# Low parts of every second w_up tile formed by an accumulating DMA in SBUF

## Chip, cores and metric

The kernel runs on one core of one Trainium2 chip. The metric is the device time of one execution in microseconds (us), from two runs of the kernel before.

## What is computed

The reference is one decoder layer in float32: x is 256 tokens of 2048 features; attention and a gated short convolution run side by side, then comes cross-attention on 256 memory tokens, a squared-ReLU MLP and a final norm. The change lies in the MLP's first product:

```
u = jax.nn.relu(rms_norm(x, norm_mlp) @ w_up)      # w_up: 2048 x 8192
x = x + (u * u) @ w_down                           # w_down: 8192 x 2048
```

The inputs and the weights are float32, and the output has to be near a float32 result.

## The kernel before

TensorE multiplies in the format float32r (F32R), which keeps fewer bits than float32. So each operand is split: a high part, which is the value rounded to F32R, and a low part, which is what the rounding left. A product is then formed from three matmuls: high by high, high by low, low by high.

Weights stream from HBM. `weights` (L70) loads a tile of 256 rows by 512 columns (512 KB; in SBUF 128 partitions by 1024 elements) with one DMA from SP's queue (`load_w`, L54 to L59) into a buffer `raw`, and splits it (`split_w`, L61 to L68): ScalarE writes `whi`, the rounded weights (L66), and VectorE writes `wlo` = raw - whi (L67). There are six `raw` buffers and five each of `whi` and `wlo` (L40, L41). A buffer is filled anew when the last reader of its former content is done. SP's queue issues the loads in order, so a load that waits for its buffer holds back those behind it.

The MLP works in four passes (L468). Each first forms 2048 of the 8192 hidden features with w_up, in four groups of 512 columns (`feat_group`, L84 to L94), and then multiplies them with 2048 rows of w_down into the token-major residual (`tok_group`, L107 to L114), four groups again. In `feat_group` the contraction over 2048 rows runs in four steps of four k tiles (L87): two tiles of weights are loaded and split (L88), and for each of four blocks of 128 output features four k tiles go through `feat_step`. Here the weights are the operand that TensorE loads, and the activations move through. For each k one matmul has the high weights and 512 columns, the activations' high and low parts side by side (L78), and one has the low weights and 256 columns (L79); for a group's last k the order is turned round (L81, L82). At a group's end ScalarE and VectorE evacuate each block as it is finished (`ev_u`, L473 to L479), square it and split it for the next product.

So w_up takes 16 groups of four steps, and each step uses two loaded tiles, which `split_w` returns as four (high, low) pairs. The framework puts in the semaphores, and orders each engine's instructions by its own simulated schedule.

Of the kernel before, what the change touches and what calls it, by code (L numbers as in the profile page):

```python
# [11 lines left out]
F32R = mybir.dt.float32r  # L12
AF = mybir.ActivationFunctionType
ALU = mybir.AluOpType
# [3 lines left out]
P = 128  # L18
# [16 lines left out]
def hybrid_block(ctx: ExitStack, tc: tile.TileContext, x, mem, xf, memf, cols, rope, w_in, w_attn_out,  # L35
                 w_conv_out, w_mix_out, wq_x, wkv_x, wo_x, w_up, w_down, norm_final, out):
    nc = tc.nc
# [3 lines left out]
    wsp = ctx.enter_context(tc.tile_pool(name="wsp", bufs=5))  # L41
# [5 lines left out]
    def psum_mm():  # L47
        return mm.tile([P, 512], F32, name="acc")
# [5 lines left out]
    def load_w(w, k0, nk, c0, step=2):  # L54
        raw = wraw.tile([P, nk, 512], F32, name="raw")
        for k in range(0, nk, step):
            rows = w[(k0 + k) * P:(k0 + k + step) * P, c0:c0 + 512]
            nc.sync.dma_start(raw[:, k:k + step, :], rows.rearrange("(k p) c -> p k c", p=P))
        return raw  # L59

    def split_w(raw, hi=None, lo=None, step=2):  # L61
        nk = raw.shape[1]
        hi = wsp.tile([P, nk, 512], F32R, name="whi") if hi is None else hi
        lo = wsp.tile([P, nk, 512], F32R, name="wlo") if lo is None else lo
        for k in range(0, nk, step):
            nc.scalar.activation(hi[:, k:k + step, :], raw[:, k:k + step, :], AF.Copy)  # L66
            nc.vector.tensor_sub(lo[:, k:k + step, :], raw[:, k:k + step, :], hi[:, k:k + step, :].bitcast(F32))  # L67
        return [(hi[:, k, :], lo[:, k, :]) for k in range(nk)]  # L68

    def weights(w, k0, c0):  # L70
        return split_w(load_w(w, k0, 2, c0))


    def feat_step(ps, b, k, nk, wh, wl, xs):

        a, c = wh[:, b * P:(b + 1) * P], wl[:, b * P:(b + 1) * P]
        if k < nk - 1:
            nc.tensor.matmul(ps, a, xs(k, 2), start=(k == 0), stop=False)  # L78
            nc.tensor.matmul(ps[:, S:], c, xs(k, 0), start=False, stop=False)  # L79
        else:  # L80
            nc.tensor.matmul(ps[:, S:], c, xs(k, 0), start=False, stop=False)  # L81
            nc.tensor.matmul(ps, a, xs(k, 2), start=(k == 0), stop=True)  # L82

    def feat_group(w, c0, kr0, nk, xs, evac):  # L84

        ps = [None] * 4
        for k0 in range(0, nk, 4):  # L87
            parts = weights(w, kr0 + k0, c0) + weights(w, kr0 + k0 + 2, c0)  # L88
            for b in range(4):
                ps[b] = psum_mm() if k0 == 0 else ps[b]  # L90
                for j in range(4):
                    feat_step(ps[b], b, k0 + j, nk, *parts[j], xs)
                if k0 + 4 == nk:
                    evac(b, ps[b])  # L94
# [21 lines left out]
    def parts_of(t, k0=0):  # L116

        def get(k, which):
            if which == 2:
                return t[:, k0 + k, :, :].rearrange("p a s -> p (a s)")  # L120
            return t[:, k0 + k, which, :]
        return get
# [35 lines left out]
    for q in range(8):  # L158
        raw = wraw.tile([P, 2, 512], F32, name="raw") if q < 6 else None
# [69 lines left out]
    for c in range(2):  # L229
        for i in range(2):  # L230
# [5 lines left out]
            if i == c == 0:  # L236
                ps = [psum_mm(), psum_mm()]
                for q in range(8):
                    for k in range(2):
                        split_scaled(hT, 2 * q + k, xraw[:, 2 * q + k, :], g_of(0, 2 * q + k))  # L240
                    parts = split_w(first[q] or load_w(w_in, 2 * q, 2, 0), step=1 if q < 2 else 2)
# [162 lines left out]
    for h in range(NX):  # L404
# [6 lines left out]
        for c in range(2):  # L411
            nc.scalar.activation(px[:, h, c, :], sc[:, c * S:(c + 1) * S], AF.Exp, bias=st[:, 2 + c:3 + c],
                                 scale=SCALE, accum_out=st[:, 4 + c:5 + c])
# [5 lines left out]
    for k0 in range(0, KD, 4):  # L419
        parts = weights(wkv_x, k0, 512) + weights(wkv_x, k0 + 2, 512)  # L420
# [47 lines left out]
    for g in range(NG):  # L468
        uT = big.tile([P, KG, 2, S], F32R, name="S2")
        for j in range(FG // 512):  # L470
            z = block().rearrange("p a (b s) -> p (a b) s", s=S)

            def ev_u(b, ps, j=j, uT=uT, z=z):  # L473
                nc.scalar.activation(z[:, b, :], ps[:, S:], AF.Copy)  # L474
                nc.vector.tensor_add(z[:, b, :], ps[:, :S], z[:, b, :])  # L475
                if b % 2:
                    t = z[:, b - 1:b + 1, :]
                    nc.vector.scalar_tensor_tensor(t, t, 0.0, t, op0=ALU.max, op1=ALU.mult)  # L478
                    split_act(uT, 4 * j + b - 1, t, 2)  # L479
            feat_group(w_up, g * FG + j * 512, 0, KD, parts_of(x3g), ev_u)  # L480
        for c in range(4 if g < NG - 1 else 3):
            def ev_d(h, ps, c=c, g=g):
                if g < NG - 1:
                    add_block(h, ps, c * 512, 512)
                else:
                    add_last(h, ps, c * 512, 512, c, nc.gpsimd)
            tok_group(w_down, c * 512, g * KG, KG, parts_of(uT), ev_d)
# [4 lines left out]
    c0, kr, xu = 1536, (NG - 1) * KG, parts_of(uT)  # L492
    ps = [psum_mm() for _ in range(3)]
    cuts = ((0, ps[0], 0, 512), (1, ps[1], 0, 256), (1, ps[2], 256, 256))
    for k0 in range(0, 8, 4):
        parts = weights(w_down, kr + k0, c0) + weights(w_down, kr + k0 + 2, c0)
        for h, t, o, n in cuts:
            tok_steps(t[:, :n], h, k0, KG, parts, xu, o, n)
    parts = []
# [65 lines left out]
```

## Time and profile before

| What | us |
|---|---|
| median of two runs | 1476.82 |
| lowest, highest run | 1476.53, 1477.11 |
| the profiled execution | 1476.77 |
| its span, first to last instruction | 1475.0 |

The profile tells one execution. Busy time says how long an engine worked on instructions; the time of a DMA is told by its issue on a queue, by the share of time in which the core's 16 DMA engines were busy, and by the bytes they moved. PE is TensorE's matmul, PEld its weight load, DVE is VectorE, ACT is ScalarE, POOL is GpSimd, SPq is the queue of SyncE. An idle time in square brackets at a row's end names what the engine waited for last. An engine that is idle and isn't on the path that sets the end costs nothing.

### The profile page before, as it was taken

To read this page: it belongs to the slowest core of one execution; us is meant where nothing else is said; L and a number is where in the kernel's file an instruction comes from. 1 tells how busy PE (TensorE), PEld (TensorE's weight loads), DVE (VectorE), ACT (ScalarE), POOL (GpSimd) and SP (SyncE) were. 2 spreads that over 40 slices of the span, in tenths; PEclk is the share of its full clock that TensorE was granted. 3 is DMA by queue.
4 is the path that set the end of the run, shared out by engine and by line. 5 is a ranking of instruction groups with operands and counts; after the bars stand their busy time and mean duration, and the time that the engine had idled before them with its cause. 6 is when DMAs were issued, how large, how long until landed. Compare 5 with 4: busy or idle time off the path is not lost.

```text
span 1475.0 us, 18233 instructions
## 1 busy us (share of the span) xinstructions
PE 1454.8 (99%) x7064; PEld 1222.4 (83%) x7064; DVE 820.9 (56%) x976; ACT 691.2 (47%) x905; POOL 13.6 (1%) x21
## 2 busy tenths in 40 slices
PE   6999999999999999999999999999999999999997
PEld 5888888888888888888888888888888888888886
DVE  5545555765554646654476655556545555556554
ACT  6444544454444445554564443444434443445442
POOL 0000000000000000000000000000000000000011
PEclk9999999999999999999999999999999999999999
DMA  9666655576666667655555566565565556665652
GB/s 337 193 193 180 184 165 178 170 227 190 187 196 188 186 197 230 212 192 180 172 171 185 187 198 191 182 197 180 194 200 179 193 188 191 192 191 179 198 189 85
DMA packets 145158, 281.27 MB, mean 191 GB/s; under 512 B 8880, under 2 KB 9520, under 8 KB 144944
## 3 DMA queue, kind: packets, MB, share of 16 engines
q1 hardware_dynamic: 141888, 272.66, 58.9%
q10 hardware_dynamic: 3184, 7.45, 1.5%
q8 instruction: 55, 0.90, 0.2%
q14 instruction: 31, 0.25, 0.1%
HBM read 277.98 MB, written 2.10 MB: 190 GB/s over the span
## 4 chain that ended last, share of the span: by engine, by line
PE 98%; DMA 1%; ACT 1%; issue 0%; DVE 0%; POOLq 0%; POOL 0%; DVEq 0%; SPq 0%; ACTq 0%
PE acc L104 23%; PE acc L105 23%; PE acc L103 23%; PE acc L78 15%; PE acc L79 8%; PE aps L145 1%; PE acc L82 1%; DMA tok<-in_x_dram 1%; PE acc L81 1%; DMA raw<-in_w_in_dram 0%; ACT junk L189 0%; PE aps L315 0%; PE aps L270 0%; PE aps L438 0%; PE aps L407 0%
## 5 line engine op out<-in xcount | busy, mean ns | idle before, releaser
L67 DVE TENSOR_TENSOR wlo<-raw,whi 128x1024 fp32r<-128x1024 f32 (+1 forms) x510 | 618.7, 1222 | 561.2 <-ACT whi L66 547.5
L66 ACT ACTIVATE whi<-raw 128x1024 fp32r<-128x1024 f32 (+1 forms) x510 | 532.9, 1055 | 564.1 <-PE acc L105 386.2
L103 PE MATMUL acc<-whi,S 128*128 128x512 f32 x1512 | 584.9, 388 | 11.4 <-ACT whi L66 11.4
L105 PE MATMUL acc<-whi,S 128*128 128x512 f32 x1512 | 587.9, 389 | 0.0
L104 PE MATMUL acc<-wlo,S 128*128 128x512 f32 x1512 | 586.3, 388 | 0.3 <-DVE wlo L67 0.3
L103 PEld LDWEIGHTS acc<-whi,S 128*128 128x128 f32 x1512 | 284.6, 188 | 68.8 <-ACT whi L66 12.7
L78 PE MATMUL acc<-S,whi 128*128 128x512 f32 x960 | 341.6, 398 | 0.0
L104 PEld LDWEIGHTS acc<-wlo,S 128*128 128x128 f32 x1512 | 284.5, 188 | 58.8 <-DVE wlo L67 1.6
L105 PEld LDWEIGHTS acc<-whi,S 128*128 128x128 f32 x1512 | 284.7, 188 | 56.2
L79 PE MATMUL acc<-S,wlo 128*128 128x256 f32 x960 | 269.7, 281 | 0.0
L78 PEld LDWEIGHTS acc<-S,whi 128*128 128x128 f32 x960 | 180.4, 188 | 41.3
L79 PEld LDWEIGHTS acc<-S,wlo 128*128 128x128 f32 x960 | 181.3, 189 | 3.1
L474 ACT ACTIVATE blk<-acc 128x256 f32<-128x256 f32 x64 | 24.3, 380 | 36.0 <-PE acc L82 35.8
L189 ACT ACTIVATE junk<-tok 128x512 f32<-128x512 f32 (+1 forms) x33 | 20.2, 613 | 37.7 <-DVE tok L459 23.6
L459 DVE SCALAR_TENSOR_TENSOR tok<-acc,q,tok 128x512 f32<-128x512 f32 (+1 forms) x33 | 24.1, 731 | 18.0 <-PE acc L105 18.0
L130 ACT ACTIVATE S<-blk 128x512 fp32r<-128x512 f32 x32 | 20.0, 626 | 25.7 <-DVE blk L478 25.7
L475 DVE TENSOR_TENSOR blk<-acc,blk 128x256 f32<-128x256 f32 x64 | 27.0, 422 | 8.0 <-ACT blk L474 8.0
L131 DVE TENSOR_TENSOR S<-blk,S 128x512 fp32r<-128x512 f32 x32 | 22.1, 692 | 9.9 <-ACT S L130 8.4
L82 PE MATMUL acc<-S,whi 128*128 128x512 f32 x64 | 25.6, 400 | 0.0
L478 DVE SCALAR_TENSOR_TENSOR blk<-blk 128x512 f32<-128x512 f32 x32 | 22.0, 689 | 0.6
L204 ACT ACTIVATE blk<-acc,r 128x512 f32<-128x512 f32 x18 | 12.4, 689 | 15.5 <-PE acc L105 15.5
L81 PE MATMUL acc<-S,wlo 128*128 128x256 f32 x64 | 18.1, 283 | 0.0
(127 smaller groups left out, 466.2 us busy)
## 6 DMA issues: line engine op xcount, KB each, us to landing
raw<-in_w_in_dram SPq DMA_DIRECT2D x158, 512.0 KB, 4.2
raw<-in_w_up_dram SPq DMA_DIRECT2D x128, 512.0 KB, 4.0
raw<-in_w_down_dram SPq DMA_DIRECT2D x128, 512.0 KB, 4.3
raw<-in_w_mix_out_dram SPq DMA_DIRECT2D x32, 512.0 KB, 4.9
raw<-in_w_attn_out_dram SPq DMA_DIRECT2D x16, 512.0 KB, 4.3
raw<-in_w_conv_out_dram SPq DMA_DIRECT2D x16, 512.0 KB, 4.5
raw<-in_wkv_x_dram SPq DMA_DIRECT2D x16, 512.0 KB, 4.2
raw<-in_wq_x_dram SPq DMA_DIRECT2D x8, 512.0 KB, 3.9
```

The costliest lines, as they stand in the source:

```text
L66: nc.scalar.activation(hi[:, k:k + step, :], raw[:, k:k + step, :], AF.Copy)
L67: nc.vector.tensor_sub(lo[:, k:k + step, :], raw[:, k:k + step, :], hi[:, k:k + step, :].bitcast(F32))
L78: nc.tensor.matmul(ps, a, xs(k, 2), start=(k == 0), stop=False)
L79: nc.tensor.matmul(ps[:, S:], c, xs(k, 0), start=False, stop=False)
L81: nc.tensor.matmul(ps[:, S:], c, xs(k, 0), start=False, stop=False)
L82: nc.tensor.matmul(ps, a, xs(k, 2), start=(k == 0), stop=True)
L103: nc.tensor.matmul(ps, xh, wh, start=(k == 0), stop=False)
L104: nc.tensor.matmul(ps, xh, wl, start=False, stop=False)
L105: nc.tensor.matmul(ps, xl, wh, start=False, stop=(k == nk - 1))
L459: nc.vector.scalar_tensor_tensor(t, ps, q3[:, h:h + 1], t, op0=ALU.mult, op1=ALU.add)
L474: nc.scalar.activation(z[:, b, :], ps[:, S:], AF.Copy)
L475: nc.vector.tensor_add(z[:, b, :], ps[:, :S], z[:, b, :])
```

## The change

A second way to form the two parts, `weights_added`, takes the place of `weights` for the second tile of each step of `feat_group`, that is, for every second tile of w_up. The tile is loaded as before. ScalarE first writes the rounding of the negated weights into `lo`. A DMA issued from GpSimd's queue then adds the raw weights to `lo` in SBUF, so that `lo` holds raw minus rounded; VectorE has no part in it. ScalarE writes `hi` as before, with an instruction of its own behind the negation. The first tile of each step, and all tiles of every other weight, go through `weights` as before.

```diff
+    def weights_added(w, k0, c0):
+
+        raw = load_w(w, k0, 2, c0)
+        hi = wsp.tile([P, 2, 512], F32R, name="whi")
+        lo = wsp.tile([P, 2, 512], F32R, name="wlo")
+        nc.scalar.activation(lo, raw, AF.Copy, scale=-1.0)
+        nc.gpsimd.dma_start(lo, raw, accum_op=ALU.add)
+        nc.scalar.activation(hi, raw, AF.Copy)
+        return [(hi[:, k, :], lo[:, k, :]) for k in range(2)]
+
 
     def feat_step(ps, b, k, nk, wh, wl, xs):
 
@@ -85,7 +95,7 @@
 
         ps = [None] * 4
         for k0 in range(0, nk, 4):
-            parts = weights(w, kr0 + k0, c0) + weights(w, kr0 + k0 + 2, c0)
+            parts = weights(w, kr0 + k0, c0) + weights_added(w, kr0 + k0 + 2, c0)
             for b in range(4):
```

## Rows read from the trace of the kernel before

**Rows 1.** Page, section 1: busy us, share of the span and instructions of each engine.
```profile
span 1475.0 us, 18233 instructions
PE 1454.8 (99%) x7064; PEld 1222.4 (83%) x7064; DVE 820.9 (56%) x976; ACT 691.2 (47%) x905; POOL 13.6 (1%) x21
```

**Rows 2.** Page, section 4: the chain that ended last, by engine.
```profile
PE 98%; DMA 1%; ACT 1%; issue 0%; DVE 0%; POOLq 0%; POOL 0%; DVEq 0%; SPq 0%; ACTq 0%
```

**Rows 3.** Windows view: length, busy us by engine, granted clock, DMA share, GB/s.
```profile
774.00:865.00 91.00, 91.00 (x493) 78.16 (x492) 56.18 (x66) 42.20 (x57) 0.00 (x0) 1.00 0.58 186
...
800.90:823.50 22.60, 22.60 (x130) 19.59 (x128) 13.62 (x17) 10.48 (x15) 0.00 (x0) 1.00 0.57 183
```

**Rows 4.** Timeline of ACT, 795 to 825: start us, duration us, instruction, count, idle before.
```profile
796.84 0.38 ACT L474 ACTIVATE blk<-acc 128x256 f32<-128x256 f32 x1 [0.18 <-PE acc L82]
...
801.42 0.37 ACT L474 ACTIVATE blk<-acc 128x256 f32<-128x256 f32 x1
...
805.95 2.01 ACT L66 ACTIVATE whi<-raw 128x1024 fp32r<-128x1024 f32 x2 [0.43 <-PE acc L78]
811.61 2.01 ACT L66 ACTIVATE whi<-raw 128x1024 fp32r<-128x1024 f32 x2 [3.65 <-issue]
...
819.46 0.38 ACT L474 ACTIVATE blk<-acc 128x256 f32<-128x256 f32 x1 [0.18 <-PE acc L82]
```

**Rows 5.** Timeline of PE and its weight loads, 800 to 813.6.
```profile
800.65 0.40 PE L82 MATMUL acc<-S,whi 128*128 128x512 f32 x1
800.88 0.40 PE L78 MATMUL acc<-S,whi 128*128 128x512 f32 x1
...
812.18 0.40 PE L78 MATMUL acc<-S,whi 128*128 128x512 f32 x1
...
812.89 0.19 PEld L79 LDWEIGHTS acc<-S,wlo 128*128 128x128 f32 x1
```

**Rows 6.** Timeline of DVE, 795 to 825: the two subtractions after 805.95.
```profile
807.04 2.36 DVE L67 TENSOR_TENSOR wlo<-raw,whi 128x1024 fp32r<-128x1024 f32 x2 [0.80 <-ACT whi L66]
```

**Rows 7.** Timeline of SP, 808 to 810, and all waits of SP's queue for L67.
```profile
808.30 0.37 SPq L58 DMA_DIRECT2D raw<-in_w_up_dram  x1
...
809.43 0.37 SPq L58 DMA_DIRECT2D raw<-in_w_up_dram  x1
...
SPq L58 <- DVE wlo L67: 1016.4, 431, 8.4
```

**Rows 8.** Windows of half a us behind those two issues, columns as in rows 3.
```profile
808.50:809.00 0.50, 0.50 (x4) 0.42 (x3) 0.50 (x1) 0.00 (x0) 0.00 (x0) 1.00 0.00 0
809.00:809.50 0.50, 0.50 (x5) 0.45 (x4) 0.40 (x1) 0.00 (x0) 0.00 (x0) 1.00 0.42 57
809.50:810.00 0.50, 0.50 (x5) 0.41 (x4) 0.00 (x0) 0.00 (x0) 0.00 (x0) 1.00 0.91 156
...
810.50:811.00 0.50, 0.50 (x4) 0.41 (x3) 0.00 (x0) 0.00 (x0) 0.00 (x0) 1.00 1.02 397
...
813.00:813.50 0.50, 0.50 (x5) 0.41 (x4) 0.50 (x1) 0.50 (x1) 0.00 (x0) 1.00 0.08 29
```

**Rows 9.** DMA views: w_up loads of all; packets 774 to 865; landing there.
```profile
raw<-in_w_up_dram SPq DMA_DIRECT2D x128, 512.0 KB, 4.0
...
q1 hardware_dynamic: 8733, 16.84, 57.9%
...
DMA to landing us min/median/max: 3.6/4.3/5.2
```

**Rows 10.** Lines view, 774 to 865: busy us, mean ns of one, idle before.
```profile
L67 DVE TENSOR_TENSOR wlo<-raw,whi 128x1024 fp32r<-128x1024 f32 x34 | 40.7, 1222 | 33.5 <-ACT whi L66 33.2
...
L66 ACT ACTIVATE whi<-raw 128x1024 fp32r<-128x1024 f32 x33 | 33.9, 1054 | 32.1 <-issue 27.3 <-PE acc L105 3.6 <-PE acc L78 1.3
```

**Rows 11.** POOL's own work: one line's instruction with its start, and its longest.
```profile
L197 POOL TENSOR_TENSOR rm<-rmss,mhalf x1: 688/688/688, 657.3 to 657.3; 128x2 f32<-128x2 f32 x1
...
L466 POOL TENSOR_TENSOR tok<-tok,S 128x512 f32<-128x512 f32 x6 | 8.2, 1369 | 785.1 <-ACT junk L189 785.1
```

**Rows 12.** Windows at the kernel's start, columns as in rows 3.
```profile
12.00:18.00 6.00, 2.63 (x8) 1.67 (x8) 1.57 (x3) 5.24 (x16) 0.00 (x0) 0.55 1.04 361
...
24.00:36.00 12.00, 12.00 (x54) 9.94 (x53) 10.63 (x14) 9.21 (x13) 0.00 (x0) 1.00 1.03 371
```

## Prediction

> **What bounds the kernel now.** I read the page first. The span is 1475.0 us, TensorE is busy for 1454.8 us of it, and the chain of work that ended last is TensorE for 98% [rows 1, 2]; VectorE and ScalarE are busy 56% and 47%. So taking work from VectorE can bring something only where TensorE waits for it. The windows view asks that of the stage that changes: in one group of w_up, 800.90 to 823.50, TensorE is busy for 22.60 of 22.60 us, at a granted clock of 1.00 (the 2.4 GHz level), while the DMA engines are busy 0.57 of the time [rows 3]. There is nothing to win there. The question is only whether TensorE keeps being fed.
>
> The timelines show the margin. I call the four k tiles of one pass of `feat_group`, two loaded tiles, a set. The evacuation of block 0 comes at 796.84 and one group later at 819.46 [rows 4]: 22.62 us for four sets, 5.655 us each. One set begins at 800.88, behind the last matmul of the group before [rows 5]; the second set after it begins at 812.18. Buffers are five deep and a set uses two, so the second tile of the set of 812.18 takes the buffer that the first tile of the set of 800.88 gives back shortly before that set ends. ScalarE's pair of roundings at 805.95 is just that: the first of its two activations is for the second tile of the set of 812.18, the next is for the set after [rows 4]. VectorE subtracts from 807.04, two in 2.36 us [rows 6], so the low part is there at 808.27. TensorE first loads it at 812.89, the weight load of L79 at the third k [rows 5]. The margin today is 812.89 - 808.27 = 4.6 us. The tile with this margin is the very one that the change alters.
>
> **The change part by part.** Half of the 128 loads of w_up [rows 9] are odd tiles: 64, one in each of 64 sets.
>
> Removed: 64 subtractions of 1222 ns on VectorE [rows 10], 78 us. VectorE is off the path, so this is worth nothing.
>
> Added on ScalarE: 64 negated roundings. They have the shape of the present rounding, 1054 ns [rows 10], 67 us in all. In a group ScalarE is busy 10.48 of 22.60 us [rows 3]; four more make 14.7 us, which TensorE's work covers. Behind the negation stand the same tile's rounding (805.95 plus two activations of 1.05 is 808.05, needed at 812.89), the next tile's rounding (to about 809.1, then a subtraction of 1.2, needed a set later), and at a group's end the evacuation that today starts at 801.42, about 1 us later; five accumulators leave it most of a group. I cost all these at nothing. Without the cover it would be the 67 us.
>
> Added on the DMA engines: 64 transfers from SBUF to SBUF which read 512 KB of raw weights, read 512 KB of negated high parts and write 512 KB. They are issued from POOL's queue, which does no other work between 658 us and the last group of w_down (its six products of L466 are there [rows 11]), so nothing is queued behind the wait that it gets. Two limits follow.
>
> First limit, **engine time**. With loads alone the DMA engines are busy 0.57 x 5.655 = 3.2 us per set (57.9% over a longer stretch: 3.27 us [rows 9]), 1.64 us for each of two loads. Left are 5.655 - 3.27 = 2.38 us. No row shows an adding transfer. From below, it costs the same as one load, 1.64 us, if the second read is hidden beside the first. From above, a load that runs alone shows engines 91% busy at 156 GB/s (809.5 to 810.0), against 397 GB/s with two in flight [rows 8]; two reads of 524 KB at 156 GB/s are 6.7 us. Between these I take two reads at a load's ordinary price, 3.28 us: the transfer moves two operands in for each one out, and its reads can be kept in flight as those of a load are. Then a set needs 3.27 + 3.28 = 6.55 us of the DMA engines, 0.90 us more than TensorE takes. The Trainium skill says of another use of the same adder (Collectives: The Full Stack, section "The bandwidth ceiling: the fold count and why AG ≠ RS ≠ AR") that a reducing transfer needs two source reads and so runs at half a copy's rate; by that the sum would be this one, and no run here has shown it yet.
>
> Second limit, **lateness**. The negation ends at 805.95 + 1.05 = 807.00 and the sum must have landed at 812.89: 5.9 us are free. From the issue of a load at 808.30 [rows 7] to the first bytes takes 0.7 to 1.2 us (nothing moves from 808.5 to 809.0 [rows 8]); two loads are in by about 813.0. So an add lands after 0.8 us to first bytes, its data, and some 0.3 us at the end; to that comes POOL's own preparation, which no row shows: I take 0.5 us, between nothing and the 1.37 us of its longest instruction [rows 11]. With 3.28 us of data that is 4.9 us alone. It won't be alone. SP today waits for the subtraction before it reloads a raw tile [rows 7]; for an odd tile it now waits for the add's landing, and the even tile's load stands behind it in SP's queue. So both loads start when the add lands, near 812, just as the next set's add is issued (807.00 + 5.655 = 812.66). Sharing evenly doubles the add's time at worst: 0.8 + 0.5 + 6.56 + 0.3 = 8.2 us. As the loop goes over two sets, a lateness D costs (D - 5.9)/2 per set: 1.1 us at 8.2, nothing at 4.9. The engine-time limit of 0.90 us lies inside this, at D = 7.7. The later loads themselves don't stall anything: a raw tile is wanted three sets on (805.95 + 17.0 = 822.9), ten us after 812.9, and the longest landing seen is 5.2 us [rows 9].
>
> Sum: 64 x 0.90 = 58 us, and the rest nothing. No work absorbs it, since TensorE has no idle time in these stages to give back. The profiled execution took 1476.77 us (span 1475.0 and 1.8 around it), as good as the median of 1476.82. 1477 + 58 = 1535.
>
> **The rivals.** *The add is hidden* (not slower). Place: the 42% of the DMA engines' time that is idle in w_up. If one add takes at most 2.38 us of the engines and lands within 5.9 us, nothing moves: 1477. Up to 2.84 us the cost stays under 2% (2.84 - 2.38 = 0.46 us, by 64 is 29.5 us). For it: both operands lie in SBUF, and loads at 397 GB/s [rows 8] show what the engines can carry; two reads at that rate take 2.64 us, 17 us in all, 1494. Against it: a share of 0.58 at 186 GB/s, the steady state of this stage [rows 3], is far from that rate, and the loads and the add will collide. The Trainium skill (DMA: Bandwidth & Descriptors, section "Anatomy of one DMA — SWDGE (gpsimd) path") fits a transfer issued from this queue as 2.0 us fixed plus bytes over 436 GB/s; with both reads counted an estimate by it is 4.4 us to landing and 2.4 us of data, a time of about 1478, and nothing in the trace of before tests it, as POOL issues no transfer there.
>
> *The add is far slower than two loads* (the adder, or reads that wait for one another). At the upper bound of 6.7 us a set takes 3.27 + 6.7 = 10.0 us, 64 x 4.3 = 276 us more: 1753. For it: the 0.91 busy at 156 GB/s of one transfer alone [rows 8]. Against it: a second one in flight cured that. With such stalls TensorE's clock may fall too: from 12 to 18 us, where it was busy for 2.63 of 6.00 us, the granted clock was 0.55, near the 1.2 GHz level; from 24 us, at full work, it is 1.00 [rows 12]. At 0.90 us of wait in 6.55 I expect 1.00.
>
> *A gain.* TensorE's clock and order are unchanged and it waits for nothing in w_up [rows 3], so I see no way to over 2%.
>
> **How the numbers follow.** Chances: two reads at about a load's price, 2.84 to 4.0 us each, +30 to +104 us: 0.44. Hidden or nearly so, 1474 to 1506: 0.39. Slower than 4.0 us, over 1581: 0.16. A gain: 0.01. The likeliest gives 1535, its own range 1506 to 1581. The two likely cases fill 1474 to 1581; to take in a first part of the slow one I end the range at 1592 (4.2 us an add). Over 2% faster 0.01, within 2% 0.39, slower 0.60; 2%, 29.5 us, is about what a measurement of this kernel can tell from no change.
>
> **What would show it.** Right: in w_up windows the DMA share near 1.0, TensorE idle about 0.9 us in each set, its releaser the add on `wlo` at L79, all w_down windows unchanged, time from issue to landing of the adds near 7 to 8 us. Engine time is wrong if the DMA share stays under 0.9 while TensorE waits: then lateness alone is the cause. The hidden case shows 22.6 us groups and adds that land within 5.9 us. What would make me wrong: the engine time of one add, which I have only bracketed, POOL's preparation, or another order of the negation on ScalarE, where each us later is half a us per set.

## The result and the profile after

| | before | changed |
|---|---|---|
| median, us | 1476.82 | 1496.01 |
| lowest to highest run | 1476.53 to 1477.11 | 1495.41 to 1496.61 |
| span of the profiled execution | 1475.0 | 1493.6 |
| ratio, 95% interval | | 1.013 (1.0106 to 1.0154) |

The change costs 19 us, 1.3%. It was predicted to cost 58: the sign is right and the time lies inside the range, but the size is three times too large. The prediction gave a change within 2% a chance of 0.39 only, and called 2% about what a measurement can tell; the interval here tells 1.3% plainly.

The page of the changed kernel (span; busy us, share and instructions of each engine; queues with packets, MB and share of 16 engines; chain that ended last) answers to [rows 1, 2, 9]:

```profile
span 1493.6 us, 18464 instructions
PE 1460.3 (98%) x7064; PEld 1224.7 (82%) x7064; DVE 747.6 (50%) x912; ACT 751.8 (50%) x969; POOL 70.0 (5%) x85
...
q1 hardware_dynamic: 141888, 272.66, 56.4%
q0 software_dynamic: 9216, 33.56, 12.9%
...
PE 70%; issue 23%; DMA 5%; POOL 1%; ACT 1%; DVE 0%; POOLq 0%; DVEq 0%; SPq 0%; ACTq 0%
```

That last row can't be trusted here in its shares: followed back through the adds, the chain books stretches in which TensorE worked as "issue". What can be read is the difference of the spans. TensorE's busy time rose by 5.5 us and its idle time from 20.2 (1475.0 - 1454.8) to 33.3 us (1493.6 - 1460.3), 13.1 more; together 18.6 us, the whole loss. A part of the rise in busy time is clock, as the windows view of the stretch in which w_up begins shows (busy us by engine, granted clock, DMA share, GB/s):

```profile
755.00:776.00 21.00, 19.05 (x102) 16.38 (x101) 8.31 (x16) 10.78 (x19) 1.75 (x2) 0.92 0.91 237
```

The prediction expected a granted clock of 1.00 (the 2.4 GHz level); in this stretch, in which TensorE was busy for 19.05 of 21 us, it was 0.92. By an estimate, 0.08 of 21 us is 1.7 us; the rest of the 5.5 isn't explained.

The moved work is there about as costed (78 and 67 us): VectorE 73 us less, ScalarE 61 us more. The q0 row is the 64 adds: 0.129 x 1493.6 / 64 = 3.0 us of the 16 engines each.

The waits view (engine, line, what it waited for: us in total, times, longest) tells what TensorE waits for now. The shift of ten lines turns L79 of before into L89, and L79 is now the line that issues the add:

```profile
PEld acc L89 <- DMA wlo<-raw: 21.3, 22, 2.3
...
PE acc L89 <- DMA wlo<-raw: 14.3, 16, 1.9
```

It is the add's landing, and only in about a third of the 64 sets. From the view of the line that issues the adds (instruction in POOL: min, median, max ns, first and last start; landing in us):

```profile
L79 POOL DMA_DIRECT2D wlo<-raw x64: 862/874/1052, 748.5 to 1387.5; - x64
...
DMA to landing us min/median/max: 4.7/6.2/8.8
```

The timelines of ScalarE, POOL and the weight loads show one set with a wait, to be read beside [rows 4, 5]:

```profile
955.97 1.06 ACT L80 ACTIVATE whi<-raw 128x1024 fp32r<-128x1024 f32 x1 [2.65 <-PE acc L88]
956.93 1.04 ACT L78 ACTIVATE wlo<-raw 128x1024 fp32r<-128x1024 f32 x1
...
958.38 0.87 POOL L79 DMA_DIRECT2D wlo<-raw  x1 [4.73 <-ACT wlo L78]
...
961.89 0.19 PEld L92 LDWEIGHTS acc<-S,whi 128*128 128x128 f32 x1
962.01 0.19 PEld L88 LDWEIGHTS acc<-S,whi 128*128 128x128 f32 x1
...
962.82 0.31 PEld L88 LDWEIGHTS acc<-S,whi 128*128 128x128 f32 x2
...
965.50 0.19 PEld L89 LDWEIGHTS acc<-S,wlo 128*128 128x128 f32 x1 [0.61 <-DMA wlo<-raw]
...
965.72 0.42 PEld L89 LDWEIGHTS acc<-S,wlo 128*128 128x128 f32 x2
```

Two things differ from what the prediction assumed. ScalarE writes the rounding (L80) first and the negation (L78) second (in 56 of the 64 sets), and 0.4 us pass from the end of the negation to POOL's instruction, so that the add goes out 958.38 - 955.97 = 2.4 us after ScalarE starts on the tile, not 1.05. And TensorE's order is no longer the one that is written: pairs of high products (L88 x2) run early and low products (L89 x2) late. The set after the group's last block (L92) starts with the weight load at 962.01 and asks for the added low part at 965.50 - 0.61 = 964.89, 2.9 us into the set. Before, the weight load that starts a set came at 812.07, and the low part was asked for at 812.89 [rows 5], 0.8 us later:

```profile
812.07 0.19 PEld L78 LDWEIGHTS acc<-S,whi 128*128 128x128 f32 x1
```

In 55 of the 64 sets TensorE's order is this new one or like it. The framework's schedule made it; that it does so because its simulation knows how long a transfer takes is a reading, which two runs below bear out. From ScalarE's start to the use there are now 964.89 - 955.97 = 8.9 us, against 812.89 - 805.95 = 6.9 before [rows 4, 5].

The windows view of 90 us of w_up (busy us by engine, granted clock, DMA share, GB/s) answers to [rows 3]:

```profile
940.00:1030.00 90.00, 87.71 (x495) 75.48 (x493) 33.57 (x42) 52.13 (x64) 13.07 (x15) 1.00 1.00 258
```

The DMA engines are busy all the time, as predicted. Whether that makes them the bound is what the experiments had to decide.

### The profile page after: what moved, and what is told of

It is laid out like the page before. It is cut to its first block, busy times and chain, and to the rows that moved or that the text cites. A ratio compares the mean times of both kernels' runs of the same rounds, so it can differ in the third digit from the quotient of the medians.

```text
span 1493.6 us, 18464 instructions
## 1 busy us (share of the span) xinstructions
PE 1460.3 (98%) x7064; PEld 1224.7 (82%) x7064; DVE 747.6 (50%) x912; ACT 751.8 (50%) x969; POOL 70.0 (5%) x85
## 4 chain that ended last, share of the span: by engine, by line
PE 70%; issue 23%; DMA 5%; POOL 1%; ACT 1%; DVE 0%; POOLq 0%; DVEq 0%; SPq 0%; ACTq 0%
PE acc L113 22%; PE acc L114 22%; PE acc L115 22%; DMA wlo<-raw 3%; PE acc L88 1%; PE acc L89 1%; PE aps L155 1%; DMA raw<-in_w_up_dram 1%; POOL wlo L79 1%; DMA tok<-in_x_dram 1%; ACT whi L66 0%; DMA raw<-in_w_in_dram 0%; PE acc L92 0%; DVE wlo L67 0%; PE aps L325 0%
## 5 line engine op out<-in xcount | busy, mean ns | idle before, releaser
L67 DVE TENSOR_TENSOR wlo<-raw,whi 128x1024 fp32r<-128x1024 f32 (+1 forms) x446 | 544.3, 1223 | 627.0 <-ACT whi L66 613.1
L66 ACT ACTIVATE whi<-raw 128x1024 fp32r<-128x1024 f32 (+1 forms) x446 | 469.0, 1054 | 416.3 <-PE acc L115 379.6
L88 PE MATMUL acc<-S,whi 128*128 128x512 f32 x960 | 329.4, 395 | 0.0
L89 PE MATMUL acc<-S,wlo 128*128 128x256 f32 x960 | 258.6, 284 | 14.4 <-DMA wlo<-raw 14.3
L89 PEld LDWEIGHTS acc<-S,wlo 128*128 128x128 f32 x960 | 181.6, 189 | 31.7 <-DMA wlo<-raw 21.3
L88 PEld LDWEIGHTS acc<-S,whi 128*128 128x128 f32 x960 | 172.8, 189 | 31.3
L80 ACT ACTIVATE whi<-raw 128x1024 fp32r<-128x1024 f32 x64 | 67.8, 1059 | 116.4 <-issue 62.8
L79 POOL DMA_DIRECT2D wlo<-raw x64 | 56.4, 881 | 674.0 <-ACT wlo L78 614.2
L78 ACT ACTIVATE wlo<-raw 128x1024 fp32r<-128x1024 f32 x64 | 66.8, 1043 | 15.8 <-PE acc L114 15.8
L199 ACT ACTIVATE junk<-tok 128x512 f32<-128x512 f32 (+1 forms) x33 | 20.3, 614 | 38.0 <-DVE tok L469 23.7
L92 PE MATMUL acc<-S,whi 128*128 128x512 f32 x64 | 25.4, 397 | 0.0
```

The costliest lines, as they stand in the source:

```text
L78: nc.scalar.activation(lo, raw, AF.Copy, scale=-1.0)
L79: nc.gpsimd.dma_start(lo, raw, accum_op=ALU.add)
L80: nc.scalar.activation(hi, raw, AF.Copy)
```

## The experiments

Two theories. **Engine time**: a set asks the DMA engines for more than the 5.66 us that TensorE takes. **Lateness**: the engines could carry it, but an add starts when a buffer comes free and lands after the time at which TensorE wants it. The kernel before is timed beside each group of runs, at 1476.75, 1476.9 and 1477.0 us.

**Six buffers** of `whi` and `wlo` in place of five, with the order of the matmuls left to the schedule, and with the written order (each group's matmuls held in the order of the code):

```diff
-    wsp = ctx.enter_context(tc.tile_pool(name="wsp", bufs=5))
+    wsp = ctx.enter_context(tc.tile_pool(name="wsp", bufs=6))
```

> Six buffers each of whi and wlo in place of five; every engine may prepare half a set (2.8 us) earlier. Engine-time theory: the DMA engines are asked for two loads and an add in each set, 2 x 1.49 + 3.01 = 6.0 us by the shares of the changed kernel's profile, against 5.66 us of TensorE; an earlier start can't change that: 1492 to 1500 us. Lateness theory: the adds land too late because they start when a buffer comes free; 2.8 us more covers it: 1475 to 1480 us.

> Written order of the matmuls and six buffers together. Engine-time theory: 1492 to 1500 us, as neither touches the DMA engines' work. Lateness theory: 2.8 us more lead cover a lateness of 0.7 to 1.7 us: 1475 to 1482 us.

Measured: 1483.6 us, ratio 1.0045 (1.003 to 1.006), and 1484.8 us, 1.0048 (1.0031 to 1.0065). Given six buffers, the schedule kept the written order in all 64 sets by itself, so the two runs are nearly one kernel, and the run with five buffers to set beside them is the next one, with the written order: 1537.6 us. One more buffer, half a set of lead, is worth 53 us there. If engine time set the pace, that lead could be won only once in each of the four passes, 4 x 2.8 = 11 us, so engine time isn't what bounds the kernel in written order. For the change's own 19 us the two runs decide less than their expectations say: the 11 to 12 us between 1496.0 and these is what four such head starts would give as well. Lateness had called for 1475 to 1482, so both expectations are missed and some loss is left. The waits of the second of them, and the view of the line that issues its adds (landing):

```profile
PEld acc L89 <- DMA wlo<-raw: 9.3, 7, 1.8
```

```profile
DMA to landing us min/median/max: 4.9/7.6/11.0
```

The windows view of the same run:

```profile
940.00:1030.00 90.00, 88.91 (x501) 76.82 (x500) 38.17 (x49) 53.44 (x68) 11.42 (x13) 1.00 1.00 273
```

Here the adds land later than in the change (7.6 against 6.2 us), and TensorE waits less (9.3 against 21.3 us). The DMA share is 1.00 in both, at 273 and 258 GB/s: the share alone doesn't tell whether the engines could have carried more.

**Written order of the matmuls**, five buffers; and the same done to the kernel before, as a control:

```diff
-            feat_group(w_up, g * FG + j * 512, 0, KD, parts_of(x3g), ev_u)
+            with tc.manual_schedule(engines={mybir.EngineType.PE}):
+                feat_group(w_up, g * FG + j * 512, 0, KD, parts_of(x3g), ev_u)
```

> The changed kernel with TensorE's matmuls inside each w_up group kept in the order in which they are written (high, low, k by k), as they stood before; in the changed kernel the schedule moved low products of the added tiles to later. Engine-time theory: the order of use doesn't matter, 1492 to 1500 us. Lateness theory: the low part is wanted 6.9 us after ScalarE starts on the tile; the add goes out 1.4 to 2.4 us after that start and lands 6.2 us later, 0.7 to 1.7 us late, half of it per set: 1499 to 1531 us.

> The kernel before with TensorE's matmuls of each w_up group kept in written order; a control for the pinning as such. They stood in that order already, so both theories: 1475 to 1479 us. If pinning itself costs time, it shows here, and the 1537.6 us of the pinned change would have to be lowered by it.

Measured: 1537.6 us, ratio 1.0407 (1.0391 to 1.0422), and 1476.7 us, 0.9999 (0.9989 to 1.0008). The pinning costs nothing by itself. With TensorE in the order that the prediction took for granted, the change costs 61 us. That this is near the 58 forecast is luck: it isn't engine time that costs them. The upper edge of the lateness theory was 1531, so it is a little more than that. The waits of the pinned change:

```profile
PEld acc L89 <- DMA wlo<-raw: 60.6, 41, 2.6
PE acc L89 <- DMA wlo<-raw: 46.5, 40, 2.2
```

The landing of its adds, from the view of their line:

```profile
DMA to landing us min/median/max: 4.7/6.1/8.6
```

The windows view of a stretch in w_up:

```profile
950.00:1040.00 90.00, 79.12 (x430) 66.63 (x429) 28.50 (x37) 46.67 (x58) 11.42 (x13) 0.98 0.93 231
```

This kernel is slower than the change, and its DMA engines are less busy (0.93 at 231 GB/s, against 1.00 at 258): they aren't what sets its pace.

The adds land just as they did (6.1 against 6.2 us), and 41 sets wait instead of 22. The two differ in the order of use by TensorE (with it, that of the evacuations on ScalarE and VectorE; and at 12 group ends the schedule runs four matmuls of the next group early, as the pinning holds the order within a group only). That order is worth 1537.6 - 1496.0 = 42 us.

**A copy in place of the add**, in the change's own order on every engine, and with the written order:

```diff
-        nc.gpsimd.dma_start(lo, raw, accum_op=ALU.add)
+        nc.gpsimd.dma_start(lo.bitcast(F32), raw)
```

> The transfer copies the raw weights over lo and adds nothing, so the low parts of every second tile of w_up are wrong (they hold the whole weight); all engines keep the order of the changed kernel. If the second read makes the price: engine time of a transfer falls from 3.0 to about 1.5 us, 4.5 us in a set, all hidden: 1473 to 1479 us under both theories. If the price is that of a transfer from POOL's queue as such, 3 us stay: 1492 to 1500 us.

> Written order, five buffers, and a plain copy of the raw weights over lo in place of the add, so the low parts of every second tile of w_up are wrong. Lateness theory: a copy landed after 4.6 us in the kernel with the change's own order, against 6.2 for the add; 2.4 + 4.6 - 6.9 = 0.1 us late: 1475 to 1484 us. If the price of the pinned change (1537.6 us) were POOL's queue or ScalarE's negation and not the transfer's length: above 1500 us.

Measured: 1474.6 us, ratio 0.9987 (0.9978 to 0.9997), and 1484.8 us, 1.0051 (1.0036 to 1.0066). The queue of the copies on the page of the first:

```profile
q0 software_dynamic: 9216, 33.56, 5.8%
```

The view of the line that issues them, in the same run (POOL's instruction, and the landing):

```profile
L79 POOL DMA_DIRECT2D wlo<-raw x64: 537/539/755, 748.4 to 1366.2; - x64
...
DMA to landing us min/median/max: 2.9/4.6/7.2
```

A copy takes 0.058 x 1472.0 / 64 = 1.3 us of the engines, the add 3.0. It lands 1.6 us sooner by the median, and the loss is gone; so it is the adding transfer that costs, and neither the negation nor a transfer from POOL's queue as such. Every engine has the change's order in the first run, so it also shows that the change's order of matmuls costs nothing by itself; it is even 2 us faster than before. For the second run, the waits and the landing:

```profile
PEld acc L89 <- DMA wlo<-raw: 10.9, 17, 1.5
```

```profile
DMA to landing us min/median/max: 2.8/4.3/7.8
```

In written order the lateness by medians would be about nothing (2.4 + 4.3 - 6.9), but the slowest copies land after 7.8 us, 17 sets wait, and 8 us are lost all the same (0.8 us above the expectation): late landings cost, early ones give nothing back.

**Lighter loads**, written order: for each first tile only half of the rows are loaded and used twice.

```diff
+    def weights_half(w, k0, c0):
+        raw = wraw.tile([P, 2, 512], F32, name="raw")
+        nc.sync.dma_start(raw[:, 0, :], w[k0 * P:(k0 + 1) * P, c0:c0 + 512])
+        both = raw[:, 0:1, :].to_broadcast([P, 2, 512])
...
-            parts = weights(w, kr0 + k0, c0) + weights_added(w, kr0 + k0 + 2, c0)
+            parts = weights_half(w, kr0 + k0, c0) + weights_added(w, kr0 + k0 + 2, c0)
```

> Written order of the matmuls, five buffers, and for the first tile of each w_up step only 128 of its 256 rows are loaded; they stand for the other 128 too, so half of those products are left wrong. Loads in a set fall from 1048 to 786 KB, all else as in the pinned change. If the adds land late because they share the DMA engines with the loads: landing falls from 6.1 us median towards the 4.7 us minimum, lateness 2.4 + 4.7 - 6.9 = 0.2 us, 1478 to 1495 us. If 6.1 us is what an add takes by itself: 1525 to 1540 us.

Measured: 1513.6 us, ratio 1.0244 (1.0227 to 1.0261); landing:

```profile
DMA to landing us min/median/max: 4.7/5.6/9.0
```

Between the two expectations. A quarter less of loading takes 0.5 us from the median landing and 24 of the 61 us from the loss. So sharing with the loads is a part of the lateness. The fall to 4.7 us didn't come, with half of one load taken away.

**The negation first**, in written order and in the schedule's own:

```diff
+        with tc.manual_schedule(engines={mybir.EngineType.Activation}):
             nc.scalar.activation(lo, raw, AF.Copy, scale=-1.0)
             nc.gpsimd.dma_start(lo, raw, accum_op=ALU.add)
             nc.scalar.activation(hi, raw, AF.Copy)
```

> The change with written order of the matmuls, five buffers, and ScalarE's negation kept ahead of the same tile's rounding (the schedule had put it behind). The add goes out about 1.0 us earlier. Lateness theory: half of that per set, 64 x 0.5 = 32 us less than with the rounding first: 1500 to 1510 us. A theory by which the DMA engines' time sets the pinned kernel's 1537.6 us: no change, 1533 to 1540 us.

> The change with its own (rearranged) order of the matmuls left to the schedule, and only the negation kept ahead of the rounding. Lateness theory: 1.0 us earlier takes away most of what is left of the lateness, down to the 1484 us of the kernels with six buffers: 1480 to 1488 us, if the schedule moves the matmuls as far as in the change. If it moves them less because it sees the add earlier, the gain is smaller, up to 1500 us.

Measured: 1526.1 us, ratio 1.0335 (1.0319 to 1.035), and 1499.9 us, 1.0158 (1.0138 to 1.0178). The first misses both of its expectations; the second lies at the upper edge of what its own allowed. In the first the add goes out 960.12 - 958.66 = 1.5 us after ScalarE starts (it was 2.4), but of the 32 us expected only 11 came. The landing, from the view of the line that issues the adds:

```profile
DMA to landing us min/median/max: 4.5/6.3/9.7
```

Two neighbouring stretches of it in the windows view:

```profile
840.00:850.00 10.00, 6.04 (x32) 5.01 (x31) 2.45 (x2) 3.55 (x4) 0.88 (x1) 0.94 1.00 246
850.00:860.00 10.00, 10.00 (x51) 8.54 (x50) 2.80 (x4) 2.78 (x4) 0.00 (x0) 0.89 0.70 224
```

Landing times spread further (9.7 us at most, against 8.6), and with a stretch of 6.04 us of TensorE's work in 10 the granted clock fell: 0.94 in it and 0.89 in the next ten, where TensorE was busy throughout. Over the whole run it was 0.989, against 0.997 with the rounding first. By an estimate that is at most 0.008 x 1526 = 12 of the 21 us that are missing; what took the others is open. The second kernel got a new order of matmuls as well, as the expectation allowed, so it doesn't measure the negation alone: it is not decided what an earlier negation is worth in the change's own order.

**VectorE adds**: ScalarE negates as in the change, with no transfer.

```diff
-        nc.gpsimd.dma_start(lo, raw, accum_op=ALU.add)
+        nc.vector.tensor_add(lo, raw, lo.bitcast(F32))
```

> ScalarE negates as in the change, but VectorE adds the raw weights, with no transfer. It has ScalarE's added 67 us and none of the DMA's. If ScalarE's work is covered, as costed: 1474 to 1479 us. If the additional activations in ScalarE's queue delay what TensorE waits for: 1480 us or more.

Measured: 1476.0 us, ratio 0.9994 (0.9985 to 1.0004). ScalarE's 64 activations more are hidden. With no transfer the schedule left TensorE's order as before in 52 of the 64 sets. This and the six buffers are the two runs that bear on the reading above: the order moved throughout only where a transfer and five buffers came together.

**Every tile added**, six buffers, written order:

```diff
-            parts = weights(w, kr0 + k0, c0) + weights_added(w, kr0 + k0 + 2, c0)
+            parts = weights_added(w, kr0 + k0, c0) + weights_added(w, kr0 + k0 + 2, c0)
```

> Both tiles of each step get their low parts from the adding transfer, six buffers, written order. Now the DMA engines are asked for two loads (2.9 to 3.3 us) and two adds (2.65 to 3.0 us each) in a set, 8.2 to 9.3 us against 5.66 of TensorE. Engine-time theory: 64 x 2.5 to 3.6 us more, 1640 to 1710 us, DMA share near 1.0. If transfers on two queues overlapped beyond that, below 1600 us.

Measured: 1585.5 us, ratio 1.0734 (1.0713 to 1.0756), under the 1640 of the theory and in the branch below 1600. The DMA view of 80 us in the middle of a stage (packets, MB, share):

```profile
q0 software_dynamic: 2936, 10.66, 68.1%
q1 hardware_dynamic: 5711, 11.01, 37.3%
```

The landing of its adds, from the view of their line:

```profile
DMA to landing us min/median/max: 4.5/8.9/11.2
```

Here the DMA engines are near their limit: an add goes out every 3.9 us and takes 8.9 to land, so there is always one in flight, and loads beside it. These rows give the limit: 10.66 MB are 20.3 adds of 524 KB, 11.01 MB are 21.0 loads, so a pair of an add and a load takes 80 / 20.3 = 3.9 us and a set of this kernel 7.9. By busy time an add costs 0.681 x 80 / 20.3 = 2.7 us and a load 0.373 x 80 / 21.0 = 1.4. A set of the change has one add less: an estimate of 7.9 - 2.7 = 5.2 us, or, as a pair and one load more, 3.9 + 1.4 = 5.3. Even with a load at the prediction's 1.64 it is 5.6, still under TensorE's 5.66, though with little room. That is what speaks against engine time in the change itself, and it is an estimate from a kernel with another mix of transfers. That this run is still faster than 64 x (7.9 - 5.66) = 143 us more would make it isn't settled by a run; a lead that is built up in the neighbouring w_down stages, where the loads leave room, may account for it.

## Why the prediction was wrong in size

**Nothing to win, VectorE, ScalarE: right.** VectorE's time went down by 73 us without a gain, and ScalarE's activations are hidden (the run with VectorE adding).

**Engine time: the step that failed.** The 58 us were 64 x 0.90: a set was to need 6.55 us of the DMA engines, 3.27 for two loads and 3.28 for an add, against TensorE's 5.66. By the estimate from the run with every tile added a set needs 5.2 to 5.6 us, no more than TensorE takes. The add was close (3.0 in the change, 2.7 where the queue was never empty). The load was mis-sized: it was priced at 1.64 us, the busy time of the kernel before, in which loads run alone or in twos, and the add at two such loads. With the engines kept full a load takes 1.4. The prediction's own rows had that number: from 24 to 36 us loads alone moved 371 GB/s at a share of 1.03 [rows 12], and 524 KB at that rate are 1.41 us; two of these and an add at twice as much are 5.65 us, and nothing would have been left of the 58. [rows 8], which it quoted, warned as well: a share near 1 stood beside 156 GB/s and beside 397, so the share can't be read as work. For the same reason the DMA share near 1.0, which came as forecast, proved nothing, and the test that the prediction set itself, a share under 0.9, couldn't tell the two limits apart.

**Lateness: the right mechanism, taken as the lesser limit.** Forecast were 4.9 to 8.2 us from issue to landing, and half of the excess over 5.9 per set; measured were 4.7 to 8.8 us, 6.2 by the median. POOL's own part was 0.87 us, not 0.5, and the 0.4 us ahead of it were left out. The half-per-set rule holds about: in written order 2.4 + 6.1 - 6.9 = 1.6 us late, by half and by 64 sets 51 us, against 61 measured; with lighter loads 2.4 + 5.6 - 6.9 = 1.1, 35 us, against 37. It fails for the negation first (1.5 + 6.3 - 6.9 = 0.9, 29 us, against 49), where the spread and the clock add to it.

**The order on ScalarE: named as a risk, and it came.** The negation runs second, which takes 1.0 us from the 5.9.

**What was missing: the schedule moves the use.** The prediction held TensorE's order fixed, though the kernel's order of instructions is made by a planner that sees the new transfer. It moved the use of the added parts about 2 us back in the set, which covers the median landing (2.4 + 6.2 against 8.9) and leaves the late ones: 22 waits, 19 us. This is where 42 of the 61 us went.

**The rivals.** The hidden add, given 1494 at two reads at 397 GB/s and up to 1506 in its range, describes the result best, though the adds aren't quite hidden. That its 1494 lies near the measured 1496 is luck: it came from engine time, and the loss comes from waits for late adds. The estimate from the Trainium skill (DMA: Bandwidth & Descriptors, section "Anatomy of one DMA — SWDGE (gpsimd) path") of 4.4 us to landing agrees with the fastest add, 4.7, and not with the median of 6.2 beside the loads. The rule of half a copy's rate (the Trainium skill, Collectives: The Full Stack, section "The bandwidth ceiling: the fold count and why AG ≠ RS ≠ AR") agrees roughly with 3.0 us against 1.3 for a copy in the same queue and order, a factor of 2.3.

No version here that forms the right low parts beats the kernel before by more than a measurement tells; taking work from VectorE is worth nothing while TensorE is busy throughout.

## What to carry to other kernels

Price a transfer twice, by the engines' time and by the moment it lands, and take the engines' time from a stretch where they are kept full: with one or two transfers in flight the busy share stood near 1 at less than half of the rate (156 against 397 GB/s). Where a planner orders the instructions, ask what it will move when an operand gets a slow source, before you take the use of that operand as fixed; it gave back 42 of 61 us here. And an average landing isn't enough: the late ones cost, the early ones give nothing back.

## What the runs showed of the hardware

An adding transfer of 512 KB within SBUF took 2.7 to 3.0 us of the 16 DMA engines and a plain copy 1.3; POOL spent 0.87 us on issuing the one and 0.54 on the other. The time to landing isn't a property of the transfer: 4.7 us at best, 6.2 by the median with loads beside it, 5.6 with lighter loads (in written order), 7.6 with six buffers.
